# Low parts of the queries on all 128 rows of the score products, one head after the other

## The chip, the cores and the metric

The kernel runs on one core of a Trainium2 chip. The time is device microseconds of one execution, taken as the median of several runs. The engines are named as in the profile: PE is TensorE (matmul), PEld its weight loads, DVE is VectorE, ACT is ScalarE, POOL is GpSimd, and SP is the engine whose queue issues nearly all DMA transfers.

## What is computed

The reference is one layer of a streaming encoder in float32: RMS norm, chunked attention with a learned relative-position bias, residual, RMS norm, a SwiGLU feed-forward part, residual. There are 2048 tokens, 16 heads of 64 dimensions, and a model width of 1024. The part that the change touches, cut to the core:

```python
for c in range(n_chunks):                     # chunks of 64 frames
    k0 = max(0, (c - LEFT_CHUNKS) * CHUNK)    # the chunk itself and the 8 before it
    k1 = (c + 1) * CHUNK
    q_blk = q[:, :, c * CHUNK:(c + 1) * CHUNK]
    sc = jnp.einsum('bhqd,bhkd->bhqk', q_blk, k[:, :, k0:k1]) * scale
    sc = sc + bias[None, :, :, BAND - n_keys:]
    p = jax.nn.softmax(sc, axis=-1)
    outs.append(jnp.einsum('bhqk,bhkd->bhqd', p, v[:, :, k0:k1]))
```

## The kernel before, in words

[...]

The program has three stages. `project` computes q, k and v for four sequence parts of 512 tokens; `emit_qk` (L432) splits q and k and stores them in DRAM. Attention follows, and after it the feed-forward part. What is said here is about attention.

The work of attention is 32 jobs: the four sequence parts in the order 1, 0, 2, 3 (`SEQ_OF`, L402) by eight pairs of heads. A job (`Attend`, L461) has four slots of 128 queries each. In a slot, `scores` (L507) forms q times k for both heads. Part 0 has no part before it, so its slots have 128, 256, 384 and 512 keys, in one piece. The other parts have 640 keys, which lie across the border of a PSUM bank, so that they are cut into a piece of 384 and one of 256. Each head has its own score tile of two banks, `st0` and `st1`, used anew in every slot. Two more pairs of banks go round as `ring` for transposes, for the output and for dense work that fills in.

How the parts lie on the rows matters here. The contraction is over 64 dimensions, and the array has 128 rows. For each head, k is stored with its high part on 64 rows and its low part on the other 64: for head 0 high on rows 0 to 63, for head 1 high on rows 64 to 127 (`k_d[...][heads[a ^ h], h, :]`, L447). The tile of q has three planes: planes 0 and 1 hold the high part of head 0 and of head 1, each on both halves of the rows, and plane 2 holds the low parts, head 0 on the rows 0 to 63 and head 1 on the rows 64 to 127 (L477 to L481). So L522 gets high times high plus high times low with one matmul of 128 rows, and L526 adds low times high with a matmul of 64 rows, head 0 in the one half of the array and head 1 in the other. All L522 of both heads come first, then all L526, alternating between the heads.

After the products, DVE adds the bias and takes the minimum of the negated row (L534), ACT takes the exponential (L538), DVE the reciprocal of the sum (L547) and POOL scales (L550). Three slots later PE transposes the result (L565, and the fifth block at L579); DVE and ACT copy it out of PSUM (L568, L570, L580). After four slots, `output` (L582) multiplies by v (L595), and the result is split (L601, L602).

PE's order is written out by hand (`manual_schedule`, L1528): the loop over slots at L1576 gives the transposes of slot t, the scores of slot t + 3, then projection work from `o_quarter` (L604; its matmuls are L199 to L201) as filling, then the fifth block. The projection that fills in is that of the part that was finished before, so that the first eight jobs have none. The other engines get their order from the framework's scheduler. After the scores of a job's last slot the loads of the job after the next are issued (`load`, L470) on SP's queue: three for q, one or two for k, four for the bias, and two for v in every second job. The tiles for q and k have two buffers each. The first job is loaded while `project` still runs, into tiles borrowed from there (`begin`).

Of the kernel before, what the change touches and what calls it, by code (L numbers as in the profile page):

```python
# [9 lines left out]
F32 = mybir.dt.float32  # L10
F32R = mybir.dt.float32r
# [6 lines left out]
P = 128  # L18
# [6 lines left out]
HALF = 512  # L25
# [24 lines left out]
def trunk(  # L50
# [14 lines left out]
    pe, act, dve, pool = nc.tensor, nc.scalar, nc.vector, nc.gpsimd  # L65
# [26 lines left out]
    q_d = [[dram.tile([P, 2, HALF], F32, name=f"q_{p}_{n}") for p in range(NPAIR)] for n in range(NQ)]  # L92
    k_d = [[dram.tile([P, 2, HALF], F32, name=f"k_{p}_{n}") for p in range(NPAIR)] for n in range(NQ)]
# [127 lines left out]
    def behind(w, n, lag, load, use):  # L221


        def one(k):
            def go():
                if k < n:
                    load(k)
                if k >= lag:
                    use(k - lag)

            return w * n / (n + lag), go

        return [one(k) for k in range(n + lag)]
# [14 lines left out]
    def narrow(name):  # L248
        return scratch(name)[:, :HALF]
# [110 lines left out]
    def hb_tile(n, dtype=F32R, shape=(2, 4, HALF)):  # L360

        n_ht[0] += 1
        pool_ = hp if n < 4 else phase["fp"]
        return pool_.tile([P, *shape], dtype, tag=f"hb{n}", name=f"hb{n}_{n_ht[0]}", bufs=1)
# [36 lines left out]
    heads = (slice(0, 64), slice(64, 128))  # L401
# [7 lines left out]
    def bias_tile(n, h, t=None):  # L409

        fresh = t is not None or len(bias_bufs) < 4
        if t is None:
            if fresh:
                bias_bufs.append(phase["ap"].tile([P, 640], F32, name=f"bias{h}", bufs=1))
            t = bias_bufs[(n - 2) % 4]
        if fresh:
            pool.memset(t[0:64, 0:64], -BIG)
            pool.memset(t[64:128, 576:640], -BIG)
        for n, c in enumerate((slice(64, 640), slice(0, 576))):
            e = ext_d[h : h + 1, 64 * n + c.start : 64 * n + c.start + 1]  # L420
            sp.dma_start(
                t[64 * n : 64 * n + 64, c],
                bass.AP(tensor=e.tensor, offset=e.offset, ap=[[1, 64], [1, c.stop - c.start]]),
            )
        return t
# [6 lines left out]
    def emit_qk(n, p, which, src, t=None):  # L432

        scale = (0.125, 1.0)[which]
        if t is None:
            t = narrow("t")
        dve.tensor_tensor(t, src, rows_of[n], op=ALU.mult)
        hi, lo = (narrow(m).bitcast(F32R) for m in ("hi", "lo"))
        act.activation(hi, t, AF.Copy, scale=scale)
        dve.scalar_tensor_tensor(lo, t, scale, hi.bitcast(F32), op0=ALU.mult, op1=ALU.subtract)  # L440
        for a, part in enumerate((hi, lo)):
            part = part.bitcast(F32)
            if which == 0:
                sp.dma_start(q_d[n][p][:, a, :], part)
                continue
            for h, own in enumerate(heads):
                sp.dma_start(k_d[n][p][heads[a ^ h], h, :], part[own])  # L447

    st_of, ring = [], deque()

# [10 lines left out]
    class Attend:  # L461
# [8 lines left out]
        def load(self, begin=False):  # L470
            n, p, ap = self.n, self.p, phase.get("ap")
            if begin:
                both, rest = hb_tile(2), hb_tile(3, F32)
                self.q = both[:, 0]
                self.kk = both[:, 1].rearrange("d a c -> d (a c)").rearrange("d (h c) -> d h c", h=2)
            else:
                self.q = ap.tile([P, 3, HALF], F32R, tag="q", name=f"q_{n}_{p}", bufs=2)  # L477
                self.kk = ap.tile([P, 2, 2 * HALF], F32R, tag="k", name=f"k_{n}_{p}", bufs=2)
            for half in heads:
                sp.dma_start(self.q[half, 0:2].bitcast(F32), q_d[n][p][:, 0, :].rearrange("(h d) c -> d h c", h=2))  # L480
            sp.dma_start(self.q[:, 2].bitcast(F32), q_d[n][p][:, 1, :])  # L481
            if self.prev:
                sp.dma_start(self.kk[:, :, 0:HALF].bitcast(F32), k_d[n - 1][p])
            sp.dma_start(self.kk[:, :, HALF:].bitcast(F32), k_d[n][p])
            if begin:
                flat = rest[:, 1].rearrange("d a c -> d (a c)")
                self.bias = [bias_tile(h, h, flat[:, 640 * h : 640 * h + 640]) for h in range(2)]
            else:
                self.bias = [bias_tile(2 * jobs.index(self) + h, 2 * p + h) for h in range(2)]
            if p % 2 == 0:  # L490
                here = slice(p * P, p * P + 256)
                if begin:
                    v = rest[:, 0].rearrange("d a c -> d (a c)").rearrange("d (b c) -> d b c", b=8)
                else:
                    v = ap.tile([P, 8, 256], F32, tag="v", name=f"v_{n}_{p}", bufs=2)
                if self.prev:
                    sp.dma_start(v[:, 0:4, :], v_d[n - 1][:, :, here])
                sp.dma_start(v[:, 4:8, :], v_d[n][:, :, here])
                values[n, p // 2] = v
# [7 lines left out]
        def scores(self, ib):  # L507
            ap = phase["ap"]
            q, kk = self.q, self.kk
            cols = slice(ib * P, ib * P + P)  # L510
            if self.prev:
                n, k0, cuts = 640, ib * P, (P, HALF, 768)
            else:
                n, k0, cuts = (ib + 1) * P, HALF, (0, (ib + 1) * P)
            c0 = cuts[0]
            pieces = [
                [(st_of[h], a, b, slice(k0 + a - c0, k0 + b - c0)) for a, b in zip(cuts[:-1], cuts[1:])]
                for h in range(2)
            ]
            for h in range(2):  # L520
                for st, a, b, key in pieces[h]:
                    pe.matmul(st[:, a:b], q[:, h, cols], kk[:, h, key], start=True, stop=False)  # L522
            for m in range(len(pieces[0])):
                for h, own in enumerate(heads):
                    st, a, b, key = pieces[h][m]
                    pe.matmul(st[:, a:b], q[own, 2, cols], kk[own, h, key], start=False, stop=True)  # L526
            rows = ap.tile([P, 8], F32, tag="rows", name="rows", bufs=4)
            for h in range(2):
                st = st_of[h]
                sc = ap.tile([P, 640], F32, tag="sc", name="sc", bufs=8)  # L530
                nmax = rows[:, 4 + h : 5 + h]
                t = self.bias[h]
                rev = t[:, n - 1 :: -1] if n == 640 else t[:, 0:n][:, ::-1]
                dve.tensor_tensor_reduce(  # L534
                    out=sc[:, :n], in0=st[:, c0 : c0 + n], in1=rev, scale=-1.0, scalar=3.0e38,
                    op0=ALU.add, op1=ALU.min, accum_out=nmax,
                )
                act.activation(  # L538
                    sc[:, :n], sc[:, :n], AF.Exp, bias=nmax, scale=-1.0, accum_out=rows[:, h : h + 1]
                )  # L540
                self.sc[ib, h] = sc
            self.open = (ib, rows, n)
# [717 lines left out]
    def queries_keys(g, b, big, after):  # L1260
# [13 lines left out]
        for c in range(NPAIR // 2):  # L1274
# [12 lines left out]
            def closing(pts, terms, n, p, op=ALU.subtract):  # L1287
                def go(i):
                    dve.tensor_tensor(terms[i], pts[i], terms[i], op=op)
                    emit_qk(n, p, i, terms[i], terms[i])  # L1290

                return go
# [4 lines left out]
            def t2():  # L1297
# [3 lines left out]
            steps = (  # L1301
                ("B11", lambda: pa, True, copy(pa, p1)),
                ("B21", lambda: pa, False, lambda i: emit_qk(s0, 2 * c, i, pa[i])),
                ("T1", lambda: pc, True, copy(pc, p5)),
                ("T2", t2, True, u),
# [270 lines left out]
    for t in range(slots):  # L1576
        share = left[0] / max(per - t % per - 1, 1)
        if t > 0 and t % 4 == 0:
            fill(0.5 * share)
            low = jobs[t // 4 - 1].output()  # L1580
            if t % per == 0:
                low()
                low = lambda: None
                n = t // per - 1
# [118 lines left out]
```

## Time and profile before

| what | us |
| --- | --- |
| median of 3 runs | 2396.64 |
| lowest, highest | 2394.34, 2397.82 |
| the profiled execution | 2394.31 |
| its span | 2392.5 |
| PE busy in it | 2342.1 |
| attention in it, from the first score product to the last | 486.9 to 1051.2 |

A line of the timeline has the start in microseconds from the start of the span, the time that it took, the engine, the source line, the operation, what it writes and what it reads, its shape and the count of instructions that were merged into it; in square brackets stands how long the engine was idle before it, and what ended that. A line of the waits has who waited for whom, the total in microseconds, the number of times and the longest. Matmuls are pipelined, so that one starts before the duration of the one before it has passed; the distance between two starts is the better measure.

### The profile page before, as it was taken

The page shows a single profiled execution, that of the slowest core. Times are in us where ns is not written, and L with a number is a line of the kernel's source. Part 1 is how long each engine was busy: PE and PEld are TensorE (multiplying, and loading weights), DVE is VectorE, ACT ScalarE, POOL GpSimd, SP SyncE. Part 2 cuts the span into 40 slices and gives each one's busy share as a digit, 9 for nine tenths or more (in the row PEclk, how much of TensorE's full clock was granted, in tenths as well). Part 3 has the DMA queues.
Part 4 walks back from the last instruction along what each step waited for, and adds up shares of the span by engine and source line. Part 5 has one row for each costly group of instructions (what it writes and reads, how often), then busy time and mean ns, then how long its engine had stood idle before and what let it go on. Part 6 is the DMA issues. An engine that isn't in the chain of part 4 may idle for free.

```text
span 2392.5 us, 32966 instructions
## 1 busy us (share of the span) xinstructions
PE 2342.1 (98%) x11456; PEld 1866.1 (78%) x11456; DVE 1635.7 (68%) x2618; ACT 1147.5 (48%) x2015; POOL 315.6 (13%) x422
## 2 busy tenths in 40 slices
PE   8999999989999999999999999999999999999998
PEld 6877888866666776678888888888888888888887
DVE  7776956666566666659877777677657676545577
ACT  6543643357666666656333332365433333334454
POOL 1022010034324434320000000000000000000001
PEclk9999999999999999999999999999999999999999
DMA  8799988677568977836676553577666657447664
GB/s 304 252 296 325 296 269 256 181 222 223 175 207 254 270 215 231 254 137 208 237 246 206 185 186 129 177 235 258 209 210 207 216 158 238 148 151 249 193 193 145
DMA packets 234966, 523.42 MB, mean 219 GB/s; under 512 B 26896, under 2 KB 43296, under 8 KB 230320
## 3 DMA queue, kind: packets, MB, share of 16 engines
q1 hardware_dynamic: 222896, 474.13, 61.0%
q0 software_dynamic: 11904, 47.19, 6.7%
q8 instruction: 90, 1.47, 0.3%
q14 instruction: 76, 0.62, 0.1%
HBM read 373.85 MB, written 170.44 MB: 227 GB/s over the span
## 4 chain that ended last, share of the span: by engine, by line
PE 56%; DVE 3%; DMA 1%; issue 1%; ACT 0%; SPq 0%; POOL 0%; DVEq 0%; ACTq 0%
PE pd L201 6%; PE pd L199 6%; PE pd L200 6%; PE pb L199 4%; PE pb L201 4%; PE pb L200 4%; PE pa L199 3%; PE pa L201 3%; PE pa L200 3%; PE pc L199 3%; PE pc L201 3%; PE pc L200 3%; PE tt L595 1%; PE tt L565 1%; PE tt L199 1%
## 5 line engine op out<-in xcount | busy, mean ns | idle before, releaser
L550 POOL TENSOR_SCALAR sc<-sc,rows 128x640 f32<-128x640 f32 (+4 forms) x256 | 194.6, 773 | 338.1 <-DVE rows L547 245.5
L538 ACT ACTIVATE sc<-sc,rows 128x640 f32<-128x640 f32 (+4 forms) x256 | 193.0, 756 | 75.1 <-DVE rows L534 74.5
L534 DVE CUSTOM_DVE_ANT_0 sc<-st,bias 128x640 f32<-128x640 f32 (+2 forms) x248 | 174.4, 734 | 53.8 <-issue 26.7
L199 PE MATMUL pb<-hb,w_wg_T 128*128 128x512 f32 x528 | 206.2, 390 | 4.2 <-DVE terms L1009 4.2
L201 PE MATMUL pb<-hb,w_wg_T 128*128 128x512 f32 x528 | 205.5, 389 | 0.0
L200 PE MATMUL pb<-hb,w_wg_T 128*128 128x512 f32 x528 | 205.5, 389 | 0.0
L568 DVE COPY pT<-tt 128x512 f32<-128x512 f32 (+3 forms) x128 | 81.7, 639 | 89.0 <-PE tt L565 67.8
L201 PE MATMUL pd<-a,w_d_T 128*128 128x512 f32 (+1 forms) x368 | 139.9, 380 | 0.1
L199 PE MATMUL pd<-a,w_d_T 128*128 128x512 f32 (+1 forms) x368 | 139.9, 380 | 0.0
L200 PE MATMUL pd<-a,w_d_T 128*128 128x512 f32 (+1 forms) x368 | 139.8, 380 | 0.0
L199 PE MATMUL pa<-hb,w_wg_B 128*128 128x512 f32 x352 | 136.9, 389 | 0.0
L200 PE MATMUL pa<-hb,w_wg_B 128*128 128x512 f32 x352 | 136.9, 389 | 0.0
L201 PE MATMUL pa<-hb,w_wg_B 128*128 128x512 f32 x352 | 136.9, 389 | 0.0
L565 PEld LDWEIGHTS tt<-ident,sc 128*128 128x128 f32 x928 | 106.2, 141 | 35.4 <-issue 14.0
L131 ACT ACTIVATE w_wg_T<-raw 128x1024 fp32r<-128x1024 f32 x88 | 93.0, 1058 | 78.8 <-PE pb L201 33.9
L565 PE MATMUL tt<-ident,sc 128*128 128x128 f32 x928 | 126.0, 276 | 4.1 <-ACT pT L580 4.0
L1011 ACT ACTIVATE terms<-terms 128x512 f32<-128x512 f32 x65 | 41.0, 631 | 173.9 <-DVE terms L1009 173.7
L132 DVE TENSOR_TENSOR w_wg_B<-raw,w_wg_B 128x1024 fp32r<-128x1024 f32 x66 | 80.7, 1223 | 63.4 <-ACT w_wg_B L131 63.3
L291 POOL TENSOR_TENSOR rs<-ms,neg_half 128x4 f32<-128x4 f32 (+1 forms) x7 | 7.5, 1066 | 856.5 <-DVE ms L289 856.5
L358 DVE TENSOR_TENSOR a<-raw_a,a 128x512 fp32r<-128x512 f32 x154 | 105.8, 693 | 21.2 <-ACT a L357 20.6
L199 PEld LDWEIGHTS pb<-hb,w_wg_T 128*128 128x128 f32 x528 | 99.1, 188 | 26.8 <-ACT w_wg_T L131 1.9
L595 PE MATMUL tt<-pT,v 128*64 128x512 f32 (+3 forms) x832 | 119.1, 436 | 0.1
(281 smaller groups left out, 6125.4 us busy)
## 6 DMA issues: line engine op xcount, KB each, us to landing
raw<-in_w_gu SPq DMA_DIRECT2D x77, 512.0 KB, 4.1
k<-k SPq DMA_DIRECT2D x54, 512.0 KB, 6.9
q<-q SPq DMA_DIRECT2D x93, 256.0 KB, 4.7
s_g_S<-raw POOLq DMA_DIRECT2D x44, 512.0 KB, 3.1
raw_d<-d_S SPq DMA_DIRECT2D x88, 256.0 KB, 3.6
raw_a<-aT SPq DMA_DIRECT2D x88, 256.0 KB, 3.7
raw<-s_g_S SPq DMA_DIRECT2D x44, 512.0 KB, 4.0
bias<-ext_d SPq DMA_DIRECT2D x124, 144.0 KB, 6.9
```

What stands on the lines that cost most here:

```text
L131: act.activation(hi, raw, AF.Copy)
L132: dve.tensor_tensor(lo, raw, hi.bitcast(F32), op=ALU.subtract)
L199: pe.matmul(pt, a_hi, b_hi, start=first, stop=False, skip_group_check=go_on)
L200: pe.matmul(pt, a_hi, b_lo, start=False, stop=False, skip_group_check=go_on)
L201: pe.matmul(pt, a_lo, b_hi, start=False, stop=last, skip_group_check=go_on)
L358: eng.tensor_tensor(lo, src, hi.bitcast(F32), op=ALU.subtract)
L534: dve.tensor_tensor_reduce(out=sc[:, :n], in0=st[:, c0 : c0 + n], in1=rev, scale=-1.0, scalar=3.0e38, op0=ALU.add, op1=ALU.min, accum_out= ...
L538: act.activation(sc[:, :n], sc[:, :n], AF.Exp, bias=nmax, scale=-1.0, accum_out=rows[:, h : h + 1])
L550: last_pool[0] = pool.tensor_scalar(sc[:, :n], sc[:, :n], rows[:, 2 + h : 3 + h], 1.0, op0=ALU.mult, op1=ALU.mult)
L565: pe.transpose(tt[:, u, :], sc[h][:, b * P : b * P + P], ident)
L568: dve.tensor_copy(dst, tt[:, : len(part), :])
L595: pe.matmul(po[heads[h], c0:c1], v[:, kb, c : c + 64], self.pT[:, h, r, c0:c1], start=m == 0, stop=m == len(terms) - 1,)
```

## The change

The tile of q gets a fourth plane: for each head, the high part and then the low part, each on both halves of the rows. Two transfers fill it, one for each half of the rows, in place of three. In DRAM, k has its high part on rows 0 to 63 and its low part on rows 64 to 127 for both heads. Each piece of each head then gets two matmuls of 128 rows, the high queries and at once the low queries against the same keys, so that the product of low by low is added as well. All pieces of head 0 come before those of head 1. The four banks of scores and the four banks that go round are the same as before.

```diff
@@ emit_qk @@
             for h, own in enumerate(heads):
-                sp.dma_start(k_d[n][p][heads[a ^ h], h, :], part[own])
+                sp.dma_start(k_d[n][p][heads[a], h, :], part[own])
@@ Attend.load @@
-                self.q = ap.tile([P, 3, HALF], F32R, tag="q", name=f"q_{n}_{p}", bufs=2)
+                self.q = ap.tile([P, 4, HALF], F32R, tag="q", name=f"q_{n}_{p}", bufs=2)
                 self.kk = ap.tile([P, 2, 2 * HALF], F32R, tag="k", name=f"k_{n}_{p}", bufs=2)
+            src = q_d[n][p].rearrange("(h d) a c -> d h (a c)", h=2)
             for half in heads:
-                sp.dma_start(self.q[half, 0:2].bitcast(F32), q_d[n][p][:, 0, :].rearrange("(h d) c -> d h c", h=2))
-            sp.dma_start(self.q[:, 2].bitcast(F32), q_d[n][p][:, 1, :])
+                sp.dma_start(self.q[half].rearrange("d (h a) c -> d h (a c)", h=2).bitcast(F32), src)
@@ Attend.scores @@
-            pieces = [
-                [(st_of[h], a, b, slice(k0 + a - c0, k0 + b - c0)) for a, b in zip(cuts[:-1], cuts[1:])]
-                for h in range(2)
-            ]
             for h in range(2):
-                for st, a, b, key in pieces[h]:
-                    pe.matmul(st[:, a:b], q[:, h, cols], kk[:, h, key], start=True, stop=False)
-            for m in range(len(pieces[0])):
-                for h, own in enumerate(heads):
-                    st, a, b, key = pieces[h][m]
-                    pe.matmul(st[:, a:b], q[own, 2, cols], kk[own, h, key], start=False, stop=True)
+                for a, b in zip(cuts[:-1], cuts[1:]):
+                    key = slice(k0 + a - c0, k0 + b - c0)
+                    pe.matmul(st_of[h][:, a:b], q[:, 2 * h, cols], kk[:, h, key], start=True, stop=False)
+                    pe.matmul(st_of[h][:, a:b], q[:, 2 * h + 1, cols], kk[:, h, key], start=False, stop=True)
```

## The prediction

> **What bounds the kernel now.** I began with the page (engines and their share), then cut the span into stages with the busy time by stretch, then read TensorE's order of time inside single slots, and last the waits, the load queue and the landing times.
>
> ```profile
> PE 2342.1 (98%) x11456; PEld 1866.1 (78%) x11456; DVE 1635.7 (68%) x2618; ACT 1147.5 (48%) x2015; POOL 315.6 (13%) x422
> ```
> ```profile
> 501.00:613.00 112.00, 105.17 (x737) 69.69 (x735) 73.99 (x183) 81.46 (x181) 46.54 (x58) 1.00 0.70 209
> 613.00:737.00 124.00, 120.77 (x692) 83.92 (x691) 76.43 (x234) 78.08 (x214) 38.34 (x70) 1.00 0.70 208
> 737.00:901.00 164.00, 161.25 (x1052) 115.22 (x1050) 108.58 (x235) 106.94 (x236) 69.31 (x76) 1.00 0.81 246
> 901.00:1055.00 154.00, 148.38 (x953) 106.77 (x953) 99.08 (x212) 96.00 (x211) 59.95 (x67) 0.99 0.63 193
> ```
>
> The columns of the four rows are the stretch and its length, the busy time (and instructions) of PE, of its weight loads, of DVE, ACT and POOL, then the granted clock, the DMA engines' busy share and GB/s. PE is the bound of the program, and of attention too: the rows are its four quarters (sequence parts 1, 0, 2, 3; eight head pairs of four slots each, 128 slots). DVE and ACT have over a quarter of each stretch free, and the granted clock is full. Only the first quarter shows PE idle by some per cent. The change touches the score products alone (L522, L526) and the loads of q, so everything outside attention keeps its time.
>
> The third and fourth quarters (and the first) have 640 keys a slot, in a piece of 384 and one of 256. One such slot on PE, columns start, duration, line, shape, count:
>
> ```profile
> 909.03 0.83 PE L522 MATMUL st<-k,q 128*128 128x384 f32 x4
> 909.79 0.56 PE L526 MATMUL st<-k,q 64*128 64x384 f32 x4
> 910.28 0.50 PE L199 MATMUL tt<-hb,w 128*128 128x512 f32 x1
> 910.62 0.39 PE L200 MATMUL tt<-hb,w 128*128 128x512 f32 x1
> 910.85 0.39 PE L201 MATMUL tt<-hb,w 128*128 128x512 f32 x1
> ```
> ```profile
> 909.29 0.45 PE L522 MATMUL st<-k,q 128*128 128x256 f32 x2
> ```
>
> Durations overlap, so I go by distances between starts. L200 to L201 is 0.23 us for 512 columns: 0.449 ns a column. The four high products (384, 256, 384, 256) start at 909.03, the second at 909.29: 0.26 for 384 columns that stream in 0.172, so a lead-in of 0.086 us behind the transposes. From 909.29 to 909.79 lie 896 columns, 0.402 us, and 0.098 of gap. The low products are four of 64 rows and take 0.49 us: 1280 columns would be 0.575, so head 0 and head 1 do run side by side, 640 columns or 0.287, with 0.20 of gap among and behind them. Last, L199 to L200 is 0.34 in place of 0.23: 0.11 more. So the low part costs 0.287 of streaming and 0.098 + 0.20 + 0.11 = 0.41 of gaps.
>
> **The change, part by part.** Two pairs of 64-row products become four products of 128 rows with the low queries, each behind the high product of the same piece. They no longer run side by side: 1280 columns, 0.575 us. The gaps stand where PE goes from 128 rows to 64 and back; between L522's own products, which change weights from head to head, and between L199, L200 and L201, which change weights each time, there is none. So I cost the four new products at streaming pace and the gaps at nothing. [...]
>
> Slot with 640 keys: before, L522 to L200 is 1.59, less 0.23 for L199: 1.36. After: 0.086 + 2560 x 0.449 ns = 1.236. Saved: 0.124. In the third and fourth quarters, 64 slots: **7.9 us**.
>
> [...]
>
> The second quarter has no earlier chunk: 128 to 512 keys a slot, one piece.
>
> ```profile
> 703.18 1.04 PE L565 MATMUL tt<-ident,sc 128*128 128x128 f32 x8
> 703.97 0.59 PE L522 MATMUL st<-k,q 128*128 128x384 f32 x2
> ...
> 705.20 0.39 PE L200 MATMUL tt<-hb,w 128*128 128x512 f32 x1
> ```
> ```profile
> 712.55 0.42 PE L522 MATMUL st<-k,q 128*128 128x128 f32 x2
> ...
> 713.49 0.39 PE L200 MATMUL tt<-hb,w 128*128 128x512 f32 x1
> ...
> 715.23 0.48 PE L522 MATMUL st<-k,q 128*128 128x256 f32 x2
> ...
> 716.29 0.39 PE L200 MATMUL tt<-hb,w 128*128 128x512 f32 x1
> ```
>
> From L522 to L200, less 0.23: 0.71, 0.83 and 1.00 us for 128, 256 and 384 keys. After, the lead-in and four products: 256 keys 0.546, 384 keys 0.776. For 128 columns the row that is nearest is the transposes' (eight in 0.79, 0.099 each, above the 0.057 of streaming): 0.086 + 0.396 = 0.482. Saved 0.23, 0.28 and 0.22; for 512 keys, by the same step from 256 to 384, 0.16: together 0.89 a head pair; eight pairs: **7.1 us**. With the 128-column product at streaming pace it would be 8.5.
>
> The first quarter has no projection work between its products and PE waits there:
>
> ```profile
> 515.71 0.83 PE L522 MATMUL st<-k,q 128*128 128x384 f32 x4
> ...
> 518.06 0.56 PE L522 MATMUL st<-k,q 128*128 128x384 f32 x2
> 518.80 0.56 PE L522 MATMUL st<-k,q 128*128 128x384 f32 x2 [0.19 <-DVE rows L534]
> 519.29 0.56 PE L526 MATMUL st<-k,q 64*128 64x384 f32 x4
> ...
> 520.87 0.56 PE L522 MATMUL st<-k,q 128*128 128x384 f32 x2
> ...
> 531.21 0.83 PE L522 MATMUL st<-k,q 128*128 128x384 f32 x4
> ```
> ```profile
> 519.98 0.83 DVE L534 CUSTOM_DVE_ANT_0 sc<-st,bias 128x640 f32<-128x640 f32 x1 [0.63 <-issue]
> ```
> ```profile
> PE st L522 <- DVE rows L534: 8.1, 30, 0.8
> PE tt L199 <- DVE hb L602: 6.0, 5, 2.5
> PE tt L565 <- ACT pT L580: 4.0, 4, 1.3
> ```
>
> A head pair takes 531.21 - 515.71 = 15.5 us. The first distance, unstalled, is 2.35; the second is 2.81, because head 1's banks are still being read by the pass of the slot before (L534), and PE is stopped between head 0's high products (518.06) and head 1's (518.80): 0.46 us. The pass cannot begin earlier because head 0's scores are finished only with L526, at the end of both heads. The new order cuts this loop: head 0 is complete after four products (0.575), so DVE starts on it while PE does head 1, and PE asks for head 1's banks 0.287 later. Three of four slots have this stall (the waits of PE over all of attention, last fence: 30 of them, but counted only beyond the modelled end of a product). Bounds for a pair: if the stall stays as long, 4 x 0.124 = 0.5; if all three go, 0.5 + 3 x 0.5 = 2.0. What is late next is DVE and ACT: DVE has 2.81 - 0.63 = 2.2 us of work in such a slot, PE would need 2.35 - 0.124 = 2.23, and ACT's 81.46 us over 112 (7.2 pairs, 29 slots) are 2.8 a slot, though a quarter of the time is PE's long output product, in which ACT catches up. So I expect the short slots at 2.4 to 2.6, not at 2.23, and take 1.3 a pair; seven pairs: **9.1 us** (3.5 to 14). The first pair, which runs from earlier tiles while the projection ends, I count at nothing.
>
> The loads of q: three transfers of 256 KB become two of 512.
>
> ```profile
> q<-q SPq DMA_DIRECT2D x93, 256.0 KB, 4.7
> ```
> ```profile
> 517.09 1.89 SPq L72 DMA_DIRECT2D q<-q  x3
> 519.02 1.20 SPq L72 DMA_DIRECT2D k<-k  x2
> ```
> ```profile
> DMA to landing us min/median/max: 2.2/5.4/11.0
> ```
>
> 31 pairs load 256 KB more each, 8.1 MB in all; the queue of SP issues one transfer fewer (0.63 us earlier for k, bias and v behind it). The loads at 517 follow the last scores of one pair (515.71) and are for the pair after the next, whose first scores come one unstalled slot behind the next pair's last (531.21): at 533.6. The last k is issued by 520.2; with the landing times of k (last fence) it is there at 525.6 as a median, 531.2 at the worst. 256 KB at the stretch's 209 GB/s is 1.25 us, the shorter pair takes 1.3 of the margin, the saved issue gives 0.63 back: 0.5 us are left at the worst and 6 at the median. No wait of PE in the list above is for a load. I cost it at nothing. The stores of k only go to other rows: same count, same sizes.
>
> Other waits of PE (the last two rows of the list, 10.0 us in 9 places) end with chains of ACT and DVE; where PE comes a slot's 0.124 earlier, it waits that longer: 1.1 us back.
>
> Sum: 7.9 + 7.1 + 9.1 - 1.1 = 23.0 us. The profiled execution took 2394.31 (span 2392.5), so 2371.3 for its like; it lies 2.3 under the median of 2396.64, and the forecast for the median is **2373.6 us**.
>
> **The rivals.** *The gaps stay (slower).* If the 0.41 us belong not to the change from 128 rows to 64 but to turning from high to low queries, they remain and the doubled stream is a pure loss: 96 slots x 0.287 = 27.6, and 1280 columns x 0.449 ns x 8 = 4.6, so +32: 2429 us. It decides at the end of L522's stream, and turns into a loss once more than 0.29 of the 0.41 stays. Against it: weights change without a gap everywhere else. Chance 0.05.
>
> *Loads come late (slower or nothing).* The 8.1 MB are exposed because the window of each pair shrinks: at the first quarter's 209 GB/s 39 us at most, less the 23: 2413. The third quarter at 0.81 share and 246 GB/s is the likeliest place. Against it: its eight pairs take 164 us, 20.5 each and five more than the first quarter's, and no wait for q or k. It decides where a pair's landing moves by more than 0.5 us past the worst seen. Chance 0.06, spread from no change to 2413.
>
> *The first quarter keeps its rhythm.* ACT or DVE become its bound and the stall only changes its name: 3.5 instead of 9.1: 2379.2. Chance 0.22.
>
> *PE alone bounds every slot.* The first quarter gives 14, no wait comes back: 2396.6 - 29 = 2367.5. Chance 0.12.
>
> That the change does not do what it says I leave at nothing: PE's order is the written one.
>
> **How the numbers follow.** The forecast has 0.55; with the two cases on its side 0.89. Its own range is 2368 to 2380. The range for 8 in 10 takes in the slow rhythm and PE alone, with the spread of the runs shown (2394.34 to 2397.82) and some of the late loads: 2364 to 2386. What a measurement of this kernel can tell from no change is about 0.2%, 4.8 us. Faster: 0.55 + 0.22 + 0.12 less a little for the unforeseen, 0.88; same: 0.04, from late loads; slower: 0.08.
>
> **What would show it.** Right: no product of 64 rows; in the 640-key slots, from the first score product to the second dense one, 1.47 us instead of 1.59, with no gap after the high products and 0.23 behind L199; first-quarter pairs of 14.2 instead of 15.5, with DVE's pass over head 0 starting before head 1's last product; q in 62 transfers of 512 KB. Wrong: distances of 0.2 and more between the new products of 256 columns, waits of PE for q or k, or first-quarter slots still at 2.8 behind ACT.

## The result, and the profile after

| | median, us | ratio to before, 95% interval |
| --- | --- | --- |
| before, 6 runs | 2393.54 | |
| after, 6 runs | 2403.90 | 1.0043 (1.0033 to 1.0053) |

The kernel became slower by 10.4 us, where 23 us less were forecast. The profiled execution of after took 2402.15 us, its span is 2400.4 (before: 2394.31 and 2392.5). Some 33 us have to be explained, and two things that the profile shows at once have to be held together: the new products do what was forecast, and the kernel is slower all the same.

First the engines' line of the page of after, and then its busy time by stretch, in the stretches and columns that the prediction used (PE, its weight loads, DVE, ACT, POOL; then the granted clock, the DMA engines' share, GB/s).

```profile
PE 2331.3 (97%) x11456; PEld 1910.9 (80%) x11456; DVE 1631.9 (68%) x2618; ACT 1147.0 (48%) x2015; POOL 314.4 (13%) x422
```
```profile
501.00:613.00 112.00, 105.58 (x762) 90.15 (x764) 74.78 (x193) 80.56 (x194) 48.05 (x63) 1.00 0.85 223
613.00:737.00 124.00, 120.80 (x727) 93.58 (x725) 78.50 (x236) 80.01 (x212) 42.38 (x71) 1.00 0.91 244
737.00:901.00 164.00, 149.14 (x963) 116.82 (x963) 100.55 (x217) 102.38 (x221) 61.75 (x70) 0.97 0.85 247
901.00:1055.00 154.00, 141.86 (x912) 112.05 (x910) 94.10 (x204) 93.95 (x204) 57.86 (x67) 0.97 0.72 209
```

Three things stand in these four rows. PE gets through more matmuls in the first two stretches than before (762 and 727 against 737 and 692), so there the change gains. In the third it gets through 963 against 1052, is idle for 15 of 164 us instead of 3, and its granted clock is 0.97 instead of 1.00. And the DMA engines are far busier (0.85 and 0.91 against 0.70 and 0.70 in the first two stretches), though their bytes per second rose by 7 and 17% only.

A 640-key slot of after on PE, columns start, duration, line, shape:

```profile
771.65 0.42 PE L519 MATMUL st<-k,q 128*128 128x384 f32 x1
771.91 0.34 PE L520 MATMUL st<-k,q 128*128 128x384 f32 x1
...
772.81 0.28 PE L520 MATMUL st<-k,q 128*128 128x256 f32 x1
772.92 0.39 PE L199 MATMUL tt<-hb,w 128*128 128x512 f32 x1
773.16 0.39 PE L200 MATMUL tt<-hb,w 128*128 128x512 f32 x1
```

From the first score product to the second dense one it is 773.16 - 771.65 = 1.51 us (forecast 1.47, before 1.59), with L520 0.26 behind L519, which was forecast as 0.086 of lead-in and 0.172 of stream, and 0.24 behind L199 where 0.34 stood. The products come close to what was costed: over the 640-key slots of the last two quarters the median of this distance is 1.50 us, and 1.59 in before.

The table compares the time between the starts of the first output product (L595 of before, L589 of after) of the pairs 1, 8, 16, 24 and 32, read from the timelines of PE. The kernels e5 and e14 are experiments below.

| us | before | after | e5 | e14 |
| --- | --- | --- | --- | --- |
| pairs 1 to 8 (part 1) | 108.1 | 103.7 | 99.0 | 103.6 |
| 8 to 16 (part 0) | 115.8 | 111.4 | 111.4 | 111.4 |
| 16 to 24 (part 2) | 161.2 | 173.9 | 156.9 | 174.7 |
| 24 to 32 (part 3) | 164.0 | 170.1 | 159.2 | 167.4 |

After gains 8.8 us in the first two quarters and loses 18.8 in the last two. That is 10.0 of the 10.4 us, so what stands outside attention kept its time. About half of the loss sits at one place. PE there, then DVE, then SP's queue:

```profile
782.35 0.40 PE L201 MATMUL tt<-hb,w 128*128 128x512 f32 x1
791.36 1.94 PE L559 MATMUL tt<-ident,sc 128*128 128x128 f32 x8 [8.61 <-DVE pT L562]
792.95 0.67 PE L519 MATMUL st<-k,q 128*128 128x384 f32 x1
```
```profile
776.35 0.97 DVE L267 TENSOR_TENSOR osum<-osum,sq 128x512 f32<-128x512 f32 x1 [0.80 <-ACT sq L266]
789.86 0.75 DVE L1187 SCALAR_TENSOR_TENSOR y<-y,gt,osum 128x512 f32<-128x512 f32 x1 [12.53 <-DMA y<-o]
790.53 0.68 DVE L562 COPY pT<-tt 128x512 f32<-128x512 f32 x1
```
```profile
761.98 0.33 SPq L72 DMA_DIRECT2D res<-in_x  x1
772.33 0.32 SPq L72 DMA_DIRECT2D x<-y  x1
772.70 1.26 SPq L72 DMA_DIRECT2D q<-q  x2
774.00 1.26 SPq L72 DMA_DIRECT2D k<-k  x2
775.36 2.68 SPq L72 DMA_DIRECT2D bias<-ext_d  x4
778.08 2.40 SPq L72 DMA_DIRECT2D v<-v  x2
781.12 0.32 SPq L72 DMA_DIRECT2D y<-o  x1
```
```profile
SPq L72 <- POOL y L1190: 9.9, 1, 9.9
```

Read them from the bottom. SP stands for 9.9 us before the store `x<-y`, which needs POOL's result of L1190. Everything behind it on the queue waits too: the loads of the next pair (1 MB of q, 1 MB of k, 0.6 MB of bias, 1 MB of v) and, behind those 3.6 MB, the load `y<-o` of 256 KB, issued at 781.12. DVE's step L1187 waits 12.53 us for it, till 789.86, 8.7 us behind its issue. On DVE the copy L562 stands behind L1187, and PE's transposes need that copy to free their banks: 8.61 us of idle PE. Then the eight transposes take 792.95 - 791.36 = 1.59 us to the next product, where eight took 0.79 before: PE comes out of the stall at half the clock (the last three columns are the granted clock, the DMA share and GB/s).

```profile
791.40:794.60 3.20, 3.20 (x14) 3.20 (x15) 1.78 (x5) 1.58 (x2) 0.61 (x1) 0.50 1.03 405
```

ACT stood in the same stall. It waits 13.35 us, till 793.02, for `raw<-in_w_o`, a load of weights issued at 786.19 on the same queue, behind the same loads. The other stops of PE of more than 1 us in these two quarters of after are of 2.60, 1.83, 3.62, 4.41 and 3.47 us, at 776, 845, 954, 964 and 979 us.

Before has the same instructions in another order, but for the third load of q. Its four `y<-o` go out ahead of the next pair's loads:

```profile
745.77 5.17 SPq L72 DMA_DIRECT2D y<-o  x4
751.20 0.87 SPq L72 DMA_DIRECT2D raw<-in_w_o  x2
759.55 1.90 SPq L72 DMA_DIRECT2D q<-q  x3
```

Apart from the loads of q, none of these instructions is touched by the diff. The built programs, compared instruction by instruction, tell why: the written order of PE and the order in which the kernel's code emits the other engines' work are the same, but the framework's scheduler laid out the engines anew. DVE's instructions stand elsewhere in 434 of 2362 places, ACT's in 411 of 1741, SP's in 286 of 1529. This is SP's queue from the third pair's loads of part 2, in the order of the built programs:

```
before: q x3, k x2, bias x4, v, y<-o x4, raw x2, q x3 ...
after:  q x2, k x2, bias x4, v x2, raw x2, q x2, k x2, bias x4,
        o<-y, y<-o, res, y<-o, res, y<-o, res, x<-y,
        q x2, k x2, bias x4, v x2, y<-o, ...
```

### The profile page after: what moved, and what is told of

The parts are those of the page before. It is cut to its first block, busy times and chain, and to the rows that moved or that the text cites. A ratio compares the mean times of both kernels' runs of the same rounds, so it can differ in the third digit from the quotient of the medians.

```text
span 2400.4 us, 32904 instructions
## 1 busy us (share of the span) xinstructions
PE 2331.3 (97%) x11456; PEld 1910.9 (80%) x11456; DVE 1631.9 (68%) x2618; ACT 1147.0 (48%) x2015; POOL 314.4 (13%) x422
## 3 DMA queue, kind: packets, MB, share of 16 engines
q8 instruction: 90, 1.47, 0.2%
## 4 chain that ended last, share of the span: by engine, by line
PE 66%; DVE 3%; DMA 3%; ACT 1%; issue 1%; POOL 0%; SPq 0%; DVEq 0%; POOLq 0%; ACTq 0%
PE pd L201 6%; PE pd L199 6%; PE pd L200 6%; PE pb L199 5%; PE pb L200 4%; PE pb L201 4%; PE tt L589 3%; PE pa L199 3%; PE pa L200 3%; PE pa L201 3%; PE pc L199 3%; PE pc L200 3%; PE pc L201 3%; PE tt L559 3%; PE tt L199 2%; PE st L519 2%
## 5 line engine op out<-in xcount | busy, mean ns | idle before, releaser
L199 PE MATMUL pb<-hb,w_wg_T 128*128 128x512 f32 x528 | 206.1, 390 | 3.6 <-DVE terms L1003 3.6
L528 DVE CUSTOM_DVE_ANT_0 sc<-st,bias 128x640 f32<-128x640 f32 (+2 forms) x248 | 174.0, 733 | 17.6 <-issue 7.1
L519 PE MATMUL st<-k,q 128*128 128x384 f32 (+3 forms) x432 | 143.7, 343 | 11.7 <-DVE rows L528 10.7
L562 DVE COPY pT<-tt 128x512 f32<-128x512 f32 (+3 forms) x128 | 81.4, 636 | 90.5 <-PE tt L559 63.9
L199 PE MATMUL pd<-a,w_d_T 128*128 128x512 f32 (+1 forms) x368 | 139.9, 380 | 0.0
L199 PE MATMUL pa<-hb,w_wg_B 128*128 128x512 f32 x352 | 136.9, 389 | 0.0
L520 PE MATMUL st<-k,q 128*128 128x384 f32 (+3 forms) x432 | 127.8, 315 | 0.0
L589 PE MATMUL tt<-pT,v 128*64 128x512 f32 (+3 forms) x832 | 121.1, 436 | 0.1
```

The lines of the kernel that those rows point to most:

```text
L199: pe.matmul(pt, a_hi, b_hi, start=first, stop=False, skip_group_check=go_on)
L519: pe.matmul(st_of[h][:, a:b], q[:, 2 * h, cols], kk[:, h, key], start=True, stop=False)
L520: pe.matmul(st_of[h][:, a:b], q[:, 2 * h + 1, cols], kk[:, h, key], start=False, stop=True)
L528: dve.tensor_tensor_reduce(out=sc[:, :n], in0=st[:, c0 : c0 + n], in1=rev, scale=-1.0, scalar=3.0e38, op0=ALU.add, op1=ALU.min, accum_out= ...
L589: pe.matmul(po[heads[h], c0:c1], v[:, kb, c : c + 64], self.pT[:, h, r, c0:c1], start=m == 0, stop=m == len(terms) - 1,)
```

## The experiments

The theories. **Order:** the loss comes from the order that the scheduler made, and the new products and loads would be faster than before in the order of before. **Loads:** it comes from the loads themselves, two of 512 KB to 64 rows each, which hold the DMA engines longer (their share is 0.85 and 0.91 in the first two stretches of after, where before has 0.70). **Products:** the forecast gain of the products is not there. The change has these three parts, and each can be had alone.

To hold the order fixed, a function at the end of `trunk` adds an edge without a semaphore between each instruction of DVE, ACT, POOL and SP and the next in the other kernel's order. It adds nothing to execute:

```diff
+    for a, b in zip(order, order[1:]):          # order: places in the other kernel's program
+        tc.add_manual_dep(mine[b], mine[a].name, mybir.DependencyInfo(NoSync, DATA), reason="order")
```

Ratios are to the kernel before in runs on the same chip, whose medians were 2393.67 to 2396.84.

### Each part by itself

**e1_new_in_old_order**: the changed kernel, with the order of before on all four engines.

> The changed kernel whole, with its products and its loads of q, but DVE, ACT, POOL and SP issue their instructions in the order of the kernel before (only the third load of q of each pair falls out of it). Theory A, the loads: the two 64-row transfers of 512 KB keep the DMA engines about 1.7 us longer for each head pair, so that other loads of the queue land late whatever the order: about 2404, as the changed kernel, and at best 2395. Theory B, the order: the framework has put the late part of attention (the loads of o, the sums, the stores of x) into another order, which alone makes the long waits: about 2374.

Measured: 2384.30 us, 0.9960 (0.9947 to 0.9973). **e2_old_in_new_order** is the mirror: the kernel before, not a line of its work changed, in the order of after.

> The kernel before, products and loads, with DVE, ACT, POOL and SP in the order of the changed kernel. Theory A (loads): as the kernel before, 2394, give or take 3. Theory B (order): slower by what the change lost against its streaming gain of 19 us, that is about 2415 to 2425.

Measured: 2427.82 us, 1.0137 (1.0122 to 1.0152), or 33 us lost by order alone. The order theory holds: with the order of before the change is a gain of 0.4%, and the order of after harms the old work as well. But 0.4% is some 10 us and not 23, so the order isn't all.

**e3_products_alone**: the loads and the layout of before, with the new products in the new order on PE, the low queries taken from plane 2. The kernel takes each value of q and k as the sum of a high and a low part; on the other half of the rows plane 2 holds the low queries of the other head, so that a product of low by low of the wrong head is added; so it is too in e5, e12 and e14.

```diff
-            for m in range(len(pieces[0])): ...       # four 64-row products behind all high ones
+            for h in range(2):
+                for a, b in zip(cuts[:-1], cuts[1:]):
+                    key = slice(k0 + a - c0, k0 + b - c0)
+                    pe.matmul(st_of[h][:, a:b], q[:, h, cols], kk[:, h, key], start=True, stop=False)
+                    pe.matmul(st_of[h][:, a:b], q[:, 2, cols], kk[:, h, key], start=False, stop=True)
```

> The new products with the loads and the tile of q as before: the low product takes all 128 rows of the shared plane of low queries (so it adds the other head's low queries times this head's low keys, a term of the size of low by low). Theory A (loads): the streaming gain shows, about 2374. Theory B (order): also 2374 if the framework's order stays near that of before, more if not; 213 of 2362 places of DVE differ. A third theory, that PE's faster slots are of no use because ACT and DVE bound attention: 2390 or more.

Measured: 2369.96 us, 0.9886 (0.9871 to 0.9901). **e4_loads_alone**: the tile with four planes and its two loads, with the old products.

```diff
-                    pe.matmul(st[:, a:b], q[own, 2, cols], kk[own, h, key], start=False, stop=True)
+                    pe.matmul(st[:, a:b], q[own, 2 * h + 1, cols], kk[own, h, key], start=False, stop=True)
```

> The new loads of q (four planes, two transfers of 512 KB on 64 rows) with the 64-row products and their order as before. Theory A (loads): slower than before by what the change lost against its 19 us of streaming gain: 2415 to 2425. Theory B (order): the framework's order is near that of the changed kernel here too (181 of 2362 places of DVE differ), so about the same; the pinned runs tell the two apart. If neither loads nor order cost anything: 2394.

Measured: 2421.66 us, 1.0110 (1.0091 to 1.0130). The products theory falls: the products alone give the forecast gain, 26.9 us against the runs beside them. The loads alone are worse than the whole change, and they bring an order much like after's (DVE differs from it in 181 places, where after differs from before in 434). e3's order differs from before's in 213 places and does no harm, so the number of places says nothing.

### Products and loads in one order

**e5_products_in_old_order** and **e6_loads_in_old_order** are e3 and e4 in the order of before.

> The new products with the old loads of q (128 rows of the shared plane of low queries, so the other head's low queries times low keys are added), and DVE, ACT, POOL and SP pinned to the order of the kernel before. If products, loads and order add up: 2370, as with the order that the framework gave it. If the run of the products alone owed part of its gain to a better order: 2378 or more.

> The new loads of q with the old products, pinned to the order of the kernel before. Additive: the changed kernel in the old order is 14 us above the products alone, so 2397 + 14 = 2411, with the other 11 us of the loads-alone run (+25) owed to its order. If slower products leave the loads more room, the loads cost nothing here: 2397 to 2400.

Measured: e5 2368.65 us, 0.9900 (0.9884 to 0.9915); e6 2404.43 us, 1.0043 (1.0030 to 1.0056). Without any change of order, the loads cost 10 us with the old products and, from e5 to e1, 14 us with the new ones. Where it falls is seen in the third stretch; the first row is e5's, the second e1's.

```profile
737.00:901.00 164.00, 161.98 (x1085) 127.51 (x1080) 110.40 (x239) 108.46 (x235) 67.55 (x75) 1.00 0.80 243
```
```profile
737.00:901.00 164.00, 154.73 (x1013) 120.96 (x1012) 101.62 (x223) 103.17 (x225) 64.08 (x72) 0.99 0.90 249
```

The same order, the same products, nearly the same GB/s, but the DMA engines are busy for 0.90 instead of 0.80 of the time, and PE does 72 matmuls fewer. It reaches PE through two loads that stand behind those of q on the queue: DVE waits for `y<-o`, and ACT, longer, for `sum<-x` (in attention; e5, then e1, in each fence; total, times, longest):

```profile
DVE y L1213 <- DMA y<-o: 4.5, 4, 2.1
ACT sq L292 <- DMA sum<-x: 5.9, 5, 2.0
```
```profile
DVE y L1213 <- DMA y<-o: 14.2, 4, 5.1
ACT sq L292 <- DMA sum<-x: 19.9, 6, 6.1
```

PE's longest stop of this stretch in e1, and one that e5 doesn't have, is for that step of ACT:

```profile
PE tt L585 <- ACT sq L292: 4.5, 1, 4.5
```

In e6 it is the same: ACT waits 15.2 us for `sum<-x` in attention (before 5.5), DVE 5.8 for `y<-o` (before 1.1).

**e9b_wide_loads_own_order** and **e9_wide_loads_in_old_order** ask whether it is the bytes or the rows. They are the changed kernel with each of the two loads going to all 128 rows: as many transfers and bytes as in after, in pieces of the same 4 KB. The halves then hold different heads, so that the scores mix the two heads: the work is the same, the values are not the reference's. e9b keeps the framework's own order, e9 has that of before.

```diff
-            for half in heads:
-                sp.dma_start(self.q[half].rearrange("d (h a) c -> d h (a c)", h=2).bitcast(F32), src)
+            for h in range(2):
+                sp.dma_start(self.q[:, 2 * h : 2 * h + 2].bitcast(F32), q_d[n][p])
```

> The changed kernel in the order of the kernel before (that was 2384), but each of the two loads of q takes 512 KB to all 128 rows in place of 64: the same bytes and the same row of 4 KB. Each head's queries then stand on their own rows only, so the scores are those of other heads for a part of the products; only the time counts. If the loads cost by their rows (4 KB packets to 64 rows took 0.30 us, twice the pace of 128 rows): the loads become as cheap as before, 2369 to 2373. If they cost by their bytes (8 MB more): 2382 to 2386.

> As the run with wide loads (two loads of 512 KB to all 128 rows; each head's queries stand on their own rows only, so scores are those of other heads for a part of the products; only the time counts), but with the order that the framework itself gives: 154 places of DVE differ from the order of before, where the changed kernel differs in 434. If both costs, of the loads and of the order, come from the loads to 64 rows: 2368 to 2374. If the framework's order is harmful wherever the loads have changed at all: 2388 or more.

Measured: e9 2371.30 us, 0.9907 (0.9892 to 0.9922); e9b 2374.28 us, 0.9911 (0.9894 to 0.9927). With the order held, the cost of the loads is gone (0.9960 to 0.9907, against 0.9900 with the old loads). And the harmful order is gone with it: e9b's own order differs from before's in 154 places of DVE, and costs nothing that can be measured. So it is the 64 rows, not the bytes, that cost time, and the two 64-row transfers are also what brought the new order. Below are the load queue's totals between 480 and 1060 us, after's and then e9's (packets, MB, share of 16 engines).

```profile
q1 hardware_dynamic: 65072, 131.82, 81.4%
```
```profile
q1 hardware_dynamic: 66985, 139.59, 75.0%
```

e9 moved more in that time with a smaller share. The rates themselves are seen in short stretches that loads of one kind fill: the first row of each fence lies in loads of q to 64 rows, the second in loads of k to 128 rows; after, and then before.

```profile
520.30:521.80 1.50, 1.31 (x10) 1.31 (x11) 1.30 (x5) 1.37 (x4) 0.21 (x1) 1.00 1.03 224
523.20:524.70 1.50, 1.50 (x11) 1.08 (x11) 1.50 (x4) 1.50 (x4) 1.28 (x3) 1.00 1.05 406
```
```profile
519.80:521.30 1.50, 1.50 (x14) 1.36 (x12) 1.31 (x4) 1.29 (x3) 0.24 (x1) 1.00 1.11 235
522.20:523.70 1.50, 1.50 (x14) 1.31 (x14) 0.86 (x5) 1.25 (x4) 0.43 (x1) 1.00 1.06 403
```

The last two columns are what to see: all 16 engines count as busy in every row, but the loads to 64 rows moved 224 to 235 GB/s and those to 128 rows 403 to 406. Before, a pair loaded 512 KB of q to 64 rows and 256 KB to 128 rows, by these rates 2.2 + 0.65 = 2.9 us; now it is 1 MB to 64 rows, 4.7 us. That is an estimate of 1.8 us more a pair, 56 us for 31 pairs, of DMA engines that were busy for 0.63 to 0.81 of the four quarters before. What limits the loads to 64 rows is not shown.

### What in the order does it

**e7_new_sp_order_old** and **e8_new_engines_order_old**: the changed kernel with SP alone, and with DVE, ACT and POOL alone, in the order of before; the others are left to the scheduler.

> The changed kernel with only SP, the queue of the loads and stores, pinned to the order of the kernel before. If the harm of the order lies in SP's queue (loads of o behind stores that wait for POOL): 2384, as with all four pinned. If it lies in DVE, ACT and POOL: near 2404.

> The changed kernel with DVE, ACT and POOL pinned to the order of the kernel before and SP left to the framework. If the harm of the order lies in SP's queue: near 2404. If it lies in DVE, ACT and POOL: 2384.

Measured: e7 2408.80 us, 1.0059 (1.0046 to 1.0071); e8 2432.33 us, 1.0161 (1.0147 to 1.0175). e7 comes out near the 2404 that was expected if the harm lay in DVE, ACT and POOL, e8 fits neither of its two cases. Neither half of the old order mends the kernel by itself, and e8 is slower than the kernel with the new order whole. But the two runs don't part the halves of after's order, because the scheduler laid out the half that was left to it anew: by the traces, DVE in e7 has neither after's order nor before's, and SP's queue in e8 has not either. In e8, for one, the four `y<-o` go out together at 760.08, behind one pair's loads and ahead of the next pair's, as in before, where after sends them one by one and the first of them behind both. So whether SP's queue or the engines that wait for it carry the harm of after's order is not shown.

**e14_products_in_new_order**: e3, that is old loads and new products, in the order of after.

> The new products with the old loads, all four other engines pinned to the order of the changed kernel. If loads and order add up (loads 14 us, order 20 us): 2369 + 20 = 2389. If the order of the changed kernel hides the loads, so that it costs all of the loss by itself: 2400 or more.

Measured: 2399.44 us, 1.0023 (1.0014 to 1.0033). Against e5, with the same instructions, the order costs 1.23%, 29 us. By the table above, 4.6 us of its profile lie in the first quarter, none in the second, 17.8 in the third and 8.2 in the fourth. Its PE, DVE's wait and SP's queue show after's stall with the loads of before:

```profile
779.49 0.40 PE L227 MATMUL tt<-hb,w 128*128 128x512 f32 x1
787.21 1.94 PE L585 MATMUL tt<-ident,sc 128*128 128x128 f32 x8 [7.32 <-DVE pT L588]
788.80 0.67 PE L545 MATMUL st<-k,q 128*128 128x384 f32 x1
```
```profile
DVE y L1213 <- DMA y<-o: 17.5, 4, 11.2
```
```profile
769.52 0.32 SPq L98 DMA_DIRECT2D x<-y  x1
769.89 1.97 SPq L98 DMA_DIRECT2D q<-q  x3
...
777.58 0.35 SPq L98 DMA_DIRECT2D y<-o  x1
```

So the stall at 782 of after belongs to the order: the `y<-o` behind a pair's loads, and these behind a store that waits for POOL. With 7.32 us of idle PE and 0.8 of slow transposes it is about half of the 17.8 that e14 loses in the third quarter. The rows of the last two stretches show of what kind the rest is (e14's; e5's row of the third stretch stands above, and its fourth has 148.60 us of PE at a clock of 1.00):

```profile
737.00:901.00 164.00, 149.82 (x957) 116.19 (x957) 99.41 (x213) 100.80 (x216) 61.20 (x69) 0.96 0.76 228
901.00:1055.00 154.00, 144.16 (x933) 113.80 (x932) 95.05 (x206) 94.44 (x206) 57.53 (x66) 0.97 0.64 198
```

In the third, PE is idle for 14.2 us instead of 2.0, and 0.04 of granted clock over 164 us are 6.6 more; in the fourth, 9.8 us instead of 5.4, and 0.03 over 154 us are 4.6. As an estimate that is 18.7 and 9.1 us, against the 17.8 and 8.2 of the table: the loss is idle PE and a lower clock, and the rest of the idle time lies in stops of up to 4.92 us behind ACT and DVE. Which places of the order make each of these was not separated.

### Rows and head order

**e12_rows_alone** parts the two halves of the edit to the products: the low products take all 128 rows, but stay where they were, behind all the high products. The orders of all engines are those of before by themselves.

```diff
-                    pe.matmul(st[:, a:b], q[own, 2, cols], kk[own, h, key], start=False, stop=True)
+                    pe.matmul(st[:, a:b], q[:, 2, cols], kk[:, h, key], start=False, stop=True)
```

> The kernel before with one thing changed: the low product of each piece and head takes all 128 rows of the shared plane of low queries (adding the other head's low queries times low keys). Loads, the order of the products (high of both heads, then low of both) and the order of all engines are those of before. The prediction's terms: the gaps go in every slot, 96 x 0.124 + 7.1 = 19 us, but the first quarter keeps its stall, since no head is complete early: 2394 - 17 to 19 = 2376. If the order head by head is what brings the gain: 2385 or more. If it brings nothing: 2370, as with the products of the change.

Measured: 2381.81 us, 0.9955 (0.9941 to 0.9969): 11.9 us, about half of the products' gain. That lies between the expectation from the prediction's terms (17 to 19 us) and that for a gain of the head order alone (9 or less): both the rows and the order count. By quarters it gains 0.8, 4.0, 3.6 and 2.3. In the first quarter it gains almost nothing, and its PE there shows why:

```profile
516.57 0.56 PE L522 MATMUL st<-k,q 128*128 128x384 f32 x2
517.32 0.56 PE L522 MATMUL st<-k,q 128*128 128x384 f32 x2 [0.19 <-DVE rows L534]
517.71 0.75 PE L526 MATMUL st<-k,q 128*128 128x384 f32 x4
...
519.36 0.56 PE L522 MATMUL st<-k,q 128*128 128x384 f32 x2
```

A slot is 519.36 - 516.57 = 2.79 us (before 2.81). The stop between the two heads is 517.32 - 516.57 = 0.75, of which 0.287 is head 0's two products, so 0.46 of stall as before. The same slots in e5, where head 0 is complete before head 1 begins:

```profile
514.78 0.42 PE L545 MATMUL st<-k,q 128*128 128x384 f32 x1
...
517.07 0.42 PE L545 MATMUL st<-k,q 128*128 128x384 f32 x1
...
519.35 0.42 PE L545 MATMUL st<-k,q 128*128 128x384 f32 x1
```

They take 2.29 and 2.28, and the stall isn't there. The rows take the gaps away; the order of the heads takes the stall away.

## Why the prediction was wrong

**The step that failed** is "The change touches the score products alone (L522, L526) and the loads of q", together with "I cost it at nothing" for the loads. The first was used as if all other engines and queues kept their order ("PE's order is the written one" holds for PE alone); what the sentence concludes, that everything outside attention keeps its time, came true. The second checked the margin of q and k alone. In numbers: products -1.00% (e5); order and loads +1.43% together, either as order 1.23% (e5 to e14) and loads on top 0.20% (e14 to after), or as loads 0.60% (e5 to e1) and order 0.83% (e1 to after). In microseconds 24 are gained and 34 lost, of these 20 to 29 by order and 5 to 14 by loads. The two aren't a sum of fixed sizes: in the order of after much of what the loads would delay is already late (DVE's wait for `y<-o` is 17.5 us in e14 with the old loads, 17.9 in after).

**The terms of the sum**, against e5, which holds all else fixed:

- 640-key slots, 0.124 us each, 7.9 us for two quarters: 4.3 and 4.8 us, 9.1. The mechanism is right, the size in part by luck: the median slot goes from 1.59 to 1.49 in e5 (1.47 forecast), and 64 times 0.10 is 6.4 us. The other 2.7 lie outside these slots and weren't separated.
- Second quarter, 7.1 us: 4.4, in e5 and in after alike, or 0.55 a pair instead of 0.89. The slots themselves gain what was forecast (medians, from the first score product to the second dense one: 0.94 to 0.76, 1.06 to 0.79, 1.23 to 1.03 and 1.41 to 1.24 us, 0.82 a pair). In e5 part of it is lost again to the granted clock, 0.99 over the quarter where before has 1.00: as an estimate, 0.01 of 124 us, some 1 us. The rest of the difference wasn't separated.
- First quarter, 9.1 us, short slots "at 2.4 to 2.6, not at 2.23": 9.1 us (108.1 to 99.0), with slots at 2.28. DVE and ACT kept pace better than allowed for, and the sum is right in part by luck: four of the seven distances between pairs fall by 1.6 to 1.7 us, three by 0.6 to 1.2, where 1.3 was taken for each. In after it is 4.4 us only, and in e14 4.5 with the old loads: under the new order DVE is late again (in after PE stops four times for 1.09 us behind its L528).
- Waits that come back, 1.1 us: not seen. The two groups that were to grow go from 10.0 us in 9 places to 9.5 in 8 (e5).
- Sum, 23 us: 24 by the ratio, 25.4 by the medians (2394.07 to 2368.65). The forecast for the products held, with terms that are off by up to 2.7 us either way.
- The gaps of 0.41 us as the price of going from 128 rows to 64 and back: e12 changes the rows alone and gains 12 us, so the first rival ("the gaps stay", +32) is refuted. All four quarters gain (0.8, 4.0, 3.6 and 2.3 us), so that running the two heads side by side outweighed the gaps in none of them. What PE does in the gaps is not shown.

**The loads, point by point.** "256 KB at the stretch's 209 GB/s is 1.25 us" priced the added bytes at a mean rate, and not the change of rows for the bytes that were there already; the rate of 64-row loads makes it 1.8 (estimate above). "No wait of PE in the list above is for a load" was right, and stayed nearly so: from 501 to 1055 us of after, this is the only wait of PE for q or k.

```profile
PE st L519 <- DMA k<-k: 0.9, 1, 0.9
```

The mistake was to ask only whether q and k come in time. What stood behind them on the queue came later as well: with the order held, from e5 to e1, DVE's wait for `y<-o` went from 4.5 to 14.2 us and ACT's for `sum<-x` from 5.9 to 19.9; the prediction looked at neither. For `y<-o` before waits 1.1 us in all:

```profile
DVE y L1193 <- DMA y<-o: 1.1, 1, 1.1
```
```profile
DVE y L1187 <- DMA y<-o: 17.9, 3, 12.5
```

These two lines are DVE's waits for it in attention, before and after.

**The rival "loads come late"** named the right quarter, and its span of times (to 2413) holds the result, at a chance of 0.06. Its mechanism was a wait for q or k, and that isn't what happened; the cost of the loads by themselves is 0.4 to 0.6%, through the loads of y and x behind them. No rival had the order, which is the larger part.

**What stays open.** Why the scheduler makes so different an order from two loads of 64 rows and a harmless one from two of 128 is not shown; that it does is (e9b against after). Which instructions of the new order cost the part of the third and fourth quarters that the stall at 782 doesn't cover wasn't settled either, nor whether one queue alone would do it: in e7 and e8 the part that was left free came out in a third order.

The fastest version of those run is e3 (0.9886), and the intervals of e5, e9 and e9b overlap its own: what they share is the new products without the new 64-row loads.

## What to carry to other kernels

When a framework's scheduler orders the engines, an edit to one load can re-order all of them: compare the order of the two built programs first, and before a difference in time is explained from the edit, run the old work in the new order and the new work in the old one. Price a transfer by the rows that it reaches as well as by its bytes (224 GB/s to 64 rows and 406 to 128 in after), and check what waits behind it on its queue, not only who reads it. A gain per slot worked out from distances between starts came out within a few microseconds here (23 forecast, 24 to 25 measured, with single terms off by up to 2.7), once the order of all engines was held. And if one part of an order is pinned, look at what the scheduler made of the rest before the run is read as a test of that part.

## What the runs showed that I had not expected

The loads of q to 64 rows kept all 16 DMA engines busy (share 1.03) at 224 GB/s, where those of k to 128 rows moved 406 at 1.05: the share of busy time alone doesn't tell the two apart here, and only share and GB/s side by side do. And a stall of 8.6 us cost PE more than its own length: behind it the granted clock was 0.50 for 3.2 us, and eight transposes took 1.59 us instead of 0.79. Shorter stops did it too, but not always: in after a stop of 2.60 us was followed by 3.4 us at 0.50 (from 777.6), in before one of 2.49 us by 3.4 us at 0.51 (from 988.6), and one of 2.13 us by 3.4 us at 1.00 (from 682.2).
